# An encoder layer on one core: one x load on another queue, the squares of the next tile ahead of the scaling, and fillers re-dealt in the prelude

## The chip, the cores and the metric

The kernel runs on one core of a Trainium2 chip. A core has TensorE (matrix products and transposes, written into PSUM), VectorE and ScalarE (elementwise work and reductions), GpSimd (POOL in the profile) and SyncE (SP), which here only issues transfers. Transfers are issued on the queues of SP, ScalarE and GpSimd and are carried by 16 DMA engines. The metric is device time in microseconds for one launch, lower is better; for the kernel before it is the median of three runs.

## The reference

One layer over a sequence of 512 positions with 2048 features (`x`), conditioned on a vector `c`; all of it in float32:

```python
c_act = silu(c)
mod = c_act @ w_ada + b_ada                  # 2048 -> 3 x 2048
shift, scale, gate = split(mod, 3)
h = rms_norm(x, norm_gain) * (1 + scale) + shift
proj = h @ w_in                              # 2048 -> 7168: q, k, v, z of 8 attention and 4 retention heads
y = concat(attention(q, k, v) * silu(z), retention(q, k, v) * silu(z))
out = rms_norm(x + gate * (y @ w_out), final_gain)
```

`rms_norm` divides each position's 2048 features by the root of their mean square (plus 1e-6). The attention is a mixture of three dilated windows, the retention runs forward and backward.

## The kernel before

The 512 positions are four tiles of 128 (`t` = 0 to 3), the 2048 features 16 blocks of 128 (`k`). Products with weights run on TensorE at 32 bits in two parts: each operand is split into a rounded part and a rest, and three products (`mm3`, L89 and L91) stand for one.

The input projection needs h transposed, with features on the partitions. Features are taken in chunks of 1, 2, 2, 3, 4 and 4 blocks (`CHUNKS`); while TensorE multiplies one chunk with the weights, shift and scale of the next chunk are summed from w_ada on VectorE (`ada_pieces`, L204 and L208, loads at L197). For the first chunk, block 0 alone, there is nothing to hide this behind. That is the prelude, and the change lies in it.

The prelude does the following:

- Loads. The four x tiles (`xn`, 1 MB each; `xt` in the profile, L121) are issued on ScalarE's queue. `c`, `b_ada` and the gain go on GpSimd's. SP issues four pieces of w_ada for block 0 (`raw0`, L115, 0.5 MB each, in runs of 512 bytes), then the first weights of w_in (L510), then w_ada for the next chunk (L197).
- Fillers. `warm(n)` multiplies a square of ones with the identity n times (L353, two instructions each). The results are not used.
- Square sums. For tile t `squares_a(t)` squares the left 1024 features on ScalarE with a running sum (L300), `squares(t)` the right 1024 on VectorE (L305), adds the two sums (L308), and has GpSimd raise the mean to the power of -1/2 (L312).
- SiLU of c. `silu_c` (L271 to L275): a transpose on TensorE, the exponential on ScalarE, three operations on VectorE, the last of which writes `ct`.
- Scaling. `scaled(t, a, b)` multiplies features a to b of x tile t in place by that factor (L316, VectorE).
- Transposes. `k0_part(t)` transposes block 0 (L322, into `psk`), `turned(t, b)` four blocks (three where b = 0) into one PSUM bank (`psx`, L328), `evacuated(t, b, eng)` copies them out to `xT` (L336).
- Shift and scale of block 0. `sums0(b, i)` adds up eight products of a raw piece with `ct` (L286, 16 instructions with one column each, into `psa`); `turn_rows` transposes `b_ada` and the gain (L266) and copies them to `bg` (L267, L268); `shift_scale0` joins them (L293 to L295).
- h of block 0. `h0_sum` and `h0_low` (L345 to L349) write its two parts, and the first projection product can start (`pw`, L89).

The order on each engine is written out by hand: every instruction passed through `pin` keeps, on its engine, its place in program order. What isn't pinned is placed by a planner, which also orders the loads of the queues and shares the completion semaphores out among them. An engine's queue is in order: an instruction that waits, the issue of a load included, holds all that follow on that engine.

Of the kernel before, what the change touches and what calls it, by code (L numbers as in the profile page):

```python
# [17 lines left out]
P = 128  # L18
D = 2048
S = 512  # L20
NT = S // P
# [15 lines left out]
N_PERSIST = 2  # L37
ADA_SPAN = 0.65
TAB_SPAN = 16
WARM = 8, 6, 5, 6  # L40
LAG = 3
RAW, RAW1, WB, LOOK, LEAD, LEAD1, EB, YB = 3, 3, 3, 2, 4, 8, 1, 22
GR = 2
# [6 lines left out]
def trunk_kernel(ctx, tc, x, c, norm_gain, w_ada, b_ada, w_in, w_out, dec_f, dec_b, final_gain, out):  # L50
    nc = tc.nc
    x2, o2 = x[0], out[0]
# [9 lines left out]
    def bank(pool, nm):  # L62
        return pool.tile([P, 512], F32, tag="b", name=nm)
# [48 lines left out]
    xn = [xp.tile([P, D], F32, name=f"xt{t}") for t in range(NT)]  # L112
# [5 lines left out]
        )  # L118

    for t in range(NT):  # L120
        nc.scalar.dma_start(xn[t], x2[t * P : (t + 1) * P, :])  # L121
    nc.gpsimd.dma_start(c_row, c.rearrange("b (k p) -> (b k) p", p=P))
    for i in range(2):
        for b in range(2):
# [23 lines left out]
    pin = tc.keep_in_program_order  # L148
# [114 lines left out]
    bg = const.tile([P, 48], F32, name="bg")  # L263

    def turn_rows():
        pin(nc.tensor.transpose(ps0[:, 64:112], bg_row, ident[0:48, 0:48]))  # L266
        pin(nc.vector.tensor_copy(bg, ps0[:, 64:112]))  # L267
        pin(nc.vector.tensor_scalar_add(bg[:, 16:32], bg[:, 16:32], 1.0))  # L268

    def silu_c():  # L270
        pin(nc.tensor.transpose(ps0[:, 0:NK], c_row, ident[0:NK, 0:NK]))  # L271
        pin(nc.scalar.activation(ce, ps0[:, 0:NK], AF.Exp, scale=-1.0))
        pin(nc.vector.tensor_scalar_add(ce, ce, 1.0))
        pin(nc.vector.reciprocal(ce, ce))
        pin(nc.vector.tensor_tensor(ct, ps0[:, 0:NK], ce, op=ALU.mult))  # L275
# [3 lines left out]
    ps0 = bank(psA, "ps0")  # L279
# [3 lines left out]
    def sums0(b, i):  # L283
        for a in range(8 * i, 8 * i + 8):
            pin(
                nc.tensor.matmul(  # L286
                    psa[:, b : b + 1], raw0[b][:, a, :], ct[:, a : a + 1],
                    start=a + b == 0, stop=a == NK - 1, skip_group_check=True,
                )
            )  # L290

    def shift_scale0():
        pin(nc.vector.tensor_tensor(sv[:, 0:1], psa[:, 0:1], bg[:, 0:1], op=ALU.add))  # L293
        pin(nc.vector.tensor_tensor(av[:, 0:1], psa[:, 1:2], bg[:, NK : NK + 1], op=ALU.add))
        pin(nc.vector.tensor_tensor(av[:, 0:1], av[:, 0:1], bg[:, 32:33], op=ALU.mult))  # L295


    def squares_a(t):
        sa = aap.tile([P, 2048], F32, tag="araw", name="sqa", bufs=AR)
        marks["sq"] = pin(nc.scalar.activation(sa[:, 0:1024], xn[t][:, 0:1024], AF.Square, accum_out=ssx[:, t, 0:1]))  # L300

    def squares(t):
        sd = aap.tile([P, 1024], F32, tag="aacc", name="sqd")
        v = xn[t][:, 1024:2048]
        pin(nc.vector.tensor_tensor_reduce(sd, v, v, 1.0 / D, EPS, ALU.mult, ALU.add, ssx[:, t, 1:2]))  # L305
        ms = small.tile([P, 1], F32, tag="ms1", name="ms1", bufs=2)
        pin(
            nc.vector.scalar_tensor_tensor(  # L308
                ms, ssx[:, t, 0:1], 1.0 / D, ssx[:, t, 1:2], op0=ALU.mult, op1=ALU.add
            )  # L310
        )
        nc.gpsimd.tensor_tensor(rsx[:, t : t + 1], ms, mhalf[:, 0:1], op=ALU.pow)  # L312

    def scaled(t, a, b):
        v = xn[t][:, a:b]
        marks["sc"] = pin(nc.vector.tensor_scalar_mul(v, v, rsx[:, t : t + 1]))  # L316
# [3 lines left out]
    def k0_part(t):  # L320
        o = psk3[:, 0:P] if t == 3 else psk[:, t * P : (t + 1) * P]
        pin(nc.tensor.transpose(o, xn[t][:, 0:P], ident))  # L322

    def turned(t, b, pin=pin):
        ps = psx[t, b] = bank(psP, "psx")
        for j in range(b == 0, 4):
            k = 4 * b + j
            pin(nc.tensor.transpose(ps[:, j * P : (j + 1) * P], xn[t][:, k * P : (k + 1) * P], ident))  # L328

    def evacuated(t, b, eng):  # L330
        for i, g in enumerate(groups):
            lo, hi = max(g[0], 4 * b), min(g[-1] + 1, 4 * b + 4)
            if i and lo < hi:
                dst = xt_tiles[i][:, lo - g[0] : hi - g[0], t * P : (t + 1) * P]
                src = psx[t, b][:, (lo - 4 * b) * P : (hi - 4 * b) * P].rearrange("p (k f) -> p k f", k=hi - lo)
                marks[eng] = pin(eng(dst, src))  # L336

    act, dve = nc.scalar.copy, nc.vector.tensor_copy
# [12 lines left out]
    def warm(n):  # L351
        for _ in range(n):
            pin(nc.tensor.matmul(ps0[:, 128:256], ones, ident, start=True, stop=True))  # L353

    warm(WARM[0])
    squares_a(0)
    squares(0)
    silu_c()
    for t in range(NT):
        scaled(t, 0, P)  # L360
        k0_part(t)
        if t == 3:
            break
        scaled(t, P, 1024)
        turned(t, 0)
        turned(t, 1)
        squares_a(t + 1)
        squares(t + 1)
        if t < 2:
            warm(WARM[1 + t])  # L370
        if t == 0:
            turn_rows()
        else:
            sums0(t - 1, 0)
        evacuated(t, 0, act)
        evacuated(t, 1, act)
    for t in range(3):
        scaled(t, 1024, D)
        turned(t, 2)
        turned(t, 3)  # L380
        evacuated(t, 3, act)
        if t:
            evacuated(t - 1, 2, dve)
# [2 lines left out]
    evacuated(2, 2, dve)  # L386
    marks["conv1"] = [marks[act], marks[dve]]
    sums0(1, 1)
    warm(WARM[3])
    shift_scale0()  # L390
    A, B = slice(0, 3 * P), slice(3 * P, S)
    h0_sum(A, psk[:, A])
# [869 lines left out]
```

## Time and profile before

| | |
|---|---|
| median of three runs | 981.01 us (980.26 to 981.70) |
| the profiled execution | 980.83 us, of which the span of instructions is 979.1 us |
| TensorE busy (products / weight loads) | 949.8 / 828.9 us of the span |
| VectorE, ScalarE, GpSimd busy | 615.6, 374.5, 12.3 us |
| DMA | 141.49 MB, 145 GB/s over the span |
| mean granted TensorE clock | 0.985 |

The profile is that of one execution. Times in it count from the first instruction. A group's row has its line in the kernel, the engine, the operation, `output<-inputs` by the names of the program, the shapes and a count. In timelines the first two numbers are start and length, and brackets hold the idle time of the engine before the row and what ended it; `ACTq` or `SPq` is an engine's sequencer issuing a load. The chain of waits follows the work that ended last back in time, from each step to what released it. The granted clock is the share of TensorE's full clock that it was given. The page divides the span into 40 slices of 24.5 us; the prelude lies in the first two of them, so it is read in finer windows.

### The profile page before, as it was taken

To read this page: it belongs to the slowest core of one execution; us is meant where nothing else is said; L and a number is where in the kernel's file an instruction comes from. 1 tells how busy PE (TensorE), PEld (TensorE's weight loads), DVE (VectorE), ACT (ScalarE), POOL (GpSimd) and SP (SyncE) were. 2 spreads that over 40 slices of the span, in tenths; PEclk is the share of its full clock that TensorE was granted. 3 is DMA by queue.
4 is the path that set the end of the run, shared out by engine and by line. 5 is a ranking of instruction groups with operands and counts; after the bars stand their busy time and mean duration, and the time that the engine had idled before them with its cause. 6 is when DMAs were issued, how large, how long until landed. Compare 5 with 4: busy or idle time off the path is not lost.

```text
span 979.1 us, 14412 instructions
## 1 busy us (share of the span) xinstructions
PE 949.8 (97%) x5614; PEld 828.9 (85%) x5614; DVE 615.6 (63%) x1079; ACT 374.5 (38%) x738; POOL 12.3 (1%) x25
## 2 busy tenths in 40 slices
PE   3999899999999999999999999999999999999996
PEld 3978689787988888988998899998899988888896
DVE  1689998966968786565565556745534472535444
ACT  2374334325236554454343232422333372333321
POOL 1000000000000000000000000000000000000001
PEclk7799999999999999999999999999999999999998
DMA  9498879732562222212224625426322148234304
GB/s 332 137 298 276 291 236 327 255 105 92 170 200 80 65 66 86 65 44 86 66 76 140 210 70 173 150 66 214 109 65 89 64 162 290 86 116 142 108 1 172
DMA packets 108803, 141.49 MB, mean 145 GB/s; under 512 B 5640, under 2 KB 78008, under 8 KB 108224
## 3 DMA queue, kind: packets, MB, share of 16 engines
q1 hardware_dynamic: 106912, 134.26, 41.8%
q10 hardware_dynamic: 1728, 6.29, 1.7%
q8 instruction: 44, 0.72, 0.3%
q14 instruction: 23, 0.19, 0.1%
q0 software_dynamic: 96, 0.03, 0.0%
HBM read 136.36 MB, written 4.20 MB: 144 GB/s over the span
## 4 chain that ended last, share of the span: by engine, by line
PE 90%; DMA 4%; DVE 3%; issue 1%; ACT 1%; POOL 0%; SPq 0%; POOLq 0%; DVEq 0%; ACTq 0%
PE pp L91 24%; PE pw L91 15%; PE pp L89 12%; PE po L91 12%; PE pw L89 8%; PE po L89 6%; PE op L91 3%; PE sp L91 2%; DMA graw<-in_w_ada_dram 2%; PE op L89 2%; PE tp L721 1%; DMA raw<-in_w_ada_dram 1%; PE sp L89 1%; PE psx L328 1%; PE psa L286 1%
## 5 line engine op out<-in xcount | busy, mean ns | idle before, releaser
L489 ACT CAST whi<-raw 128x512 fp32r<-128x512 f32 (+1 forms) x289 | 175.0, 607 | 433.2 <-PE pp L91 197.8
L490 DVE TENSOR_TENSOR wlo<-raw,whi 128x512 fp32r<-128x512 f32 (+1 forms) x289 | 193.8, 671 | 212.4 <-ACT whi L489 207.8
L91 PE MATMUL pp<-wlo,hh 128*128 128x256 f32 x576 | 161.8, 281 | 0.6 <-DVE wlo L490 0.6
L89 PE MATMUL pp<-whi,hh 128*128 128x256 f32 x576 | 162.4, 282 | 0.0
L91 PE MATMUL pp<-whi,hl 128*128 128x256 f32 x576 | 161.4, 280 | 0.0
L89 PEld LDWEIGHTS pp<-whi,hh 128*128 128x128 f32 x576 | 108.4, 188 | 2.5 <-ACT sc L790 1.7
L91 PEld LDWEIGHTS pp<-wlo,hh 128*128 128x128 f32 x576 | 108.5, 188 | 1.6 <-DVE wlo L490 0.8
L91 PEld LDWEIGHTS pp<-whi,hl 128*128 128x128 f32 x576 | 108.4, 188 | 0.0
L89 PE MATMUL pw<-hh,whi 128*128 128x512 f32 x256 | 102.8, 402 | 2.4 <-DVE acc L893 1.3
L89 PE MATMUL pp<-hh,whi 128*128 128x512 f32 x256 | 101.6, 398 | 0.6 <-DVE kl L621 0.4
L91 PE MATMUL pw<-hh,wlo 128*128 128x512 f32 x256 | 101.6, 397 | 0.0
L91 PE MATMUL pp<-hh,wlo 128*128 128x512 f32 x256 | 101.5, 396 | 0.0
L91 PE MATMUL pp<-hl,whi 128*128 128x512 f32 x256 | 101.0, 394 | 0.0
L91 PE MATMUL pw<-hl,whi 128*128 128x512 f32 x256 | 100.7, 395 | 0.0
L91 PE MATMUL po<-wlo,yh 128*128 128x512 f32 (+1 forms) x252 | 92.6, 367 | 0.0
L89 PE MATMUL po<-whi,yh 128*128 128x512 f32 (+1 forms) x252 | 92.5, 367 | 0.0
L91 PE MATMUL po<-whi,yl 128*128 128x512 f32 (+1 forms) x252 | 92.5, 367 | 0.0
L208 DVE SCALAR_TENSOR_TENSOR aacc<-araw,ct,aacc 128x512 f32<-128x512 f32 (+2 forms) x75 | 75.9, 1012 | 3.5 <-DMA araw<-in_w_ada_dram 2.2
L893 DVE TENSOR_TENSOR acc<-acc,pw 128x512 f32<-128x512 f32 x100 | 66.8, 681 | 8.0 <-PE pw L91 7.6
L946 DVE SCALAR_TENSOR_TENSOR gacc<-graw,ct,gacc 128x512 f32<-128x512 f32 x60 | 44.9, 749 | 38.4 <-DMA graw<-in_w_ada_dram 37.8
L89 PEld LDWEIGHTS pw<-hh,whi 128*128 128x128 f32 x256 | 48.1, 188 | 17.8 <-DVE acc L893 4.5
L89 PEld LDWEIGHTS pp<-hh,whi 128*128 128x128 f32 x256 | 48.1, 188 | 14.1 <-ACT e L666 0.9
(227 smaller groups left out, 1573.1 us busy)
## 6 DMA issues: line engine op xcount, KB each, us to landing
raw<-in_w_in_dram SPq DMA_DIRECT2D x94, 512.0 KB, 3.7
araw<-in_w_ada_dram SPq DMA_DIRECT2D x48, 512.0 KB, 6.4
graw<-in_w_ada_dram SPq DMA_DIRECT2D x64, 256.0 KB, 2.9
raw<-in_w_out_dram SPq DMA_DIRECT2D x32, 512.0 KB, 3.5
raw<-in_w_in_dram SPq DMA_DIRECT2D x16, 384.0 KB, 3.6
araw<-in_w_ada_dram SPq DMA_DIRECT2D x16, 384.0 KB, 4.9
xt<-in_x_dram ACTq DMA_DIRECT2D x4, 1024.0 KB, 8.3
res<-in_x_dram SPq DMA_DIRECT2D x16, 256.0 KB, 6.0
```

The lines of the kernel that those rows point to most:

```text
L89: nc.tensor.matmul(o, lh, rh, start=start, stop=False, skip_group_check=True)
L91: nc.tensor.matmul(o, a, b, start=False, stop=stop and b is (rl if swap else rh), skip_group_check=True)
L208: ins = nc.vector.scalar_tensor_tensor(acc[:, :, :n], rv[:, a], ct[:, kr + a : kr + a + 1], acc[:, :, :n], op0=ALU.mult, op1=ALU.add,)
L286: nc.tensor.matmul(psa[:, b : b + 1], raw0[b][:, a, :], ct[:, a : a + 1], start=a + b == 0, stop=a == NK - 1, skip_group_check=True,)
L328: pin(nc.tensor.transpose(ps[:, j * P : (j + 1) * P], xn[t][:, k * P : (k + 1) * P], ident))
L489: c1 = nc.scalar.copy(dh, src)
L490: c2 = nc.vector.tensor_tensor(dl, src, f32(dh), op=ALU.subtract)
L721: nc.tensor.transpose(tp_[:, j * P : (j + 1) * P], pt[:, j * P : (j + 1) * P], ident)
L893: nc.vector.tensor_tensor(accs[u][i], accs[u][i], ps[i], op=ALU.add)
L946: nc.vector.scalar_tensor_tensor(st["acc"], raw, ct[:, kr : kr + 1], st["acc"], op0=ALU.mult, op1=ALU.add)
```

## The change

Four edits in the prelude, and nothing behind it:

- The second x tile is loaded on SP's queue, ahead of all that SP issued before, and no longer on ScalarE's.
- `squares` is cut in two: the squaring keeps the name, the joining of the sums and the power become `factor`. In the written order the squares of a tile now stand between `factor` and the scaling of the tile before it. The right half of tile 0 and the first block of tile 3 are scaled at the end of the third turn, before the last transposes, and the evacuations of a tile come right behind its transposes.
- The two VectorE instructions of `turn_rows` are no longer pinned.
- The fillers are five groups (9, 4, 8, 4, 4) in place of four (8, 6, 5, 6): the second now stands behind the SiLU, ahead of the first scaled tile; the third and fourth stand behind the transposes of tiles 0 and 1; the last again ahead of the shift and scale.

```diff
-WARM = 8, 6, 5, 6
+WARM = 9, 4, 8, 4, 4
...
     for t in range(NT):
-        nc.scalar.dma_start(xn[t], x2[t * P : (t + 1) * P, :])
+        (nc.sync if t == 1 else nc.scalar).dma_start(xn[t], x2[t * P : (t + 1) * P, :])
...
         pin(nc.tensor.transpose(ps0[:, 64:112], bg_row, ident[0:48, 0:48]))
-        pin(nc.vector.tensor_copy(bg, ps0[:, 64:112]))
-        pin(nc.vector.tensor_scalar_add(bg[:, 16:32], bg[:, 16:32], 1.0))
+        nc.vector.tensor_copy(bg, ps0[:, 64:112])
+        nc.vector.tensor_scalar_add(bg[:, 16:32], bg[:, 16:32], 1.0)
...
         pin(nc.vector.tensor_tensor_reduce(sd, v, v, 1.0 / D, EPS, ALU.mult, ALU.add, ssx[:, t, 1:2]))
+
+    def factor(t):
         ms = small.tile([P, 1], F32, tag="ms1", name="ms1", bufs=2)
...
     squares_a(0)
     squares(0)
     silu_c()
-    for t in range(NT):
+    warm(WARM[1])
+    squares_a(1)
+    factor(0)
+    squares(1)
+    for t in range(3):
         scaled(t, 0, P)
+        scaled(t, P, 1024)
+        factor(t + 1)
+        if t == 2:
+            scaled(0, 1024, D)
+            scaled(3, 0, P)
+        else:
+            squares_a(t + 2)
+            squares(t + 2)
         k0_part(t)
-        if t == 3:
-            break
-        scaled(t, P, 1024)
         turned(t, 0)
         turned(t, 1)
-        squares_a(t + 1)
-        squares(t + 1)
-        if t < 2:
-            warm(WARM[1 + t])
+        evacuated(t, 0, act)
+        evacuated(t, 1, act)
         if t == 0:
+            warm(WARM[2])
             turn_rows()
         else:
+            if t == 1:
+                warm(WARM[3])
             sums0(t - 1, 0)
-        evacuated(t, 0, act)
-        evacuated(t, 1, act)
+    k0_part(3)
     for t in range(3):
-        scaled(t, 1024, D)
+        if t:
+            scaled(t, 1024, D)
         turned(t, 2)
...
-    warm(WARM[3])
+    warm(WARM[4])
     shift_scale0()
```

## The prediction

> **What bounds the kernel now.** I read the page first (span 979.1 us, TensorE busy 97% of it), then the chain of waits of the stretch that the change touches, in order of time: start, length, what.
>
> ```profile
> 1.24 13.37 DMA raw<-in_w_ada_dram
> 14.61 0.02 issue
> 14.63 0.34 ACTq L121
> 14.97 0.03 issue
> 15.00 1.28 ACT L300
> ...
> 44.12 0.90 PE psx L328 x7
> ```
>
> The prelude ends where that last row ends and the first projection matmul follows, at 45.0 us. Behind it TensorE is nearly always busy, so the prelude's length is paid in full. Its first third is strange: the chain runs through a load of w_ada to an issue on ScalarE's queue, although ScalarE's first work is to square x. The timeline of that queue, in two pieces:
>
> ```profile
> 0.74 1.40 ACTq L121 DMA_DIRECT2D xt<-in_x_dram  x3
> 14.63 0.34 ACTq L121 DMA_DIRECT2D xt<-in_x_dram  x1
> ```
>
> And VectorE's, with what ended the idle time before each row:
>
> ```profile
> 6.00 1.23 DVE L305 CUSTOM_DVE_ANT_0 sqd<-xt 128x1024 f32<-128x1024 f32 x1 [5.12 <-DMA xt<-in_x_dram]
> ...
> 17.48 0.16 DVE L308 SCALAR_TENSOR_TENSOR ms<-ssx 128x1 f32<-128x1 f32 x1 [10.24 <-ACT sqa L300]
> ...
> 18.11 0.17 DVE L275 TENSOR_TENSOR ct<-ps,ce 128x16 f32<-128x16 f32 x1
> 18.39 0.88 DVE L316 TENSOR_SCALAR xt<-xt,rsx 128x128 f32<-128x128 f32 x2
> 19.18 1.22 DVE L305 CUSTOM_DVE_ANT_0 sqd<-xt 128x1024 f32<-128x1024 f32 x1
> 20.33 0.08 DVE L305 DVE_READ_ACCUMULATOR2_ANT ssx<- 128x1 f32 x1
> ...
> 23.95 0.21 DVE L267 COPY bg<-ps 128x48 f32<-128x48 f32 x1 [3.28 <-PE ps L266]
> ...
> 27.22 0.88 DVE L316 TENSOR_SCALAR xt<-xt,rsx 128x128 f32<-128x128 f32 x2 [0.66 <-POOL rsx L312]
> ```
>
> Three x tiles are issued by 2.14. The fourth is held until 14.63, when the second raw load has landed, and everything on ScalarE is queued behind that issue. VectorE has its half of tile 0 at 6.00 and then waits 10.24 us for ScalarE's half. Why a load of x waits for one of w_ada: in the trace's issue records the loads of the two queues take eight completion semaphores in turn, and the fourth x load is the first there to reuse one still in flight.
>
> From 19.3 us TensorE, in the order written, carries the prelude. Its timeline:
>
> ```profile
> 19.32 1.76 PE L328 MATMUL psx<-ident,xt 128*128 128x128 f32 x7
> 20.87 2.77 PE L353 MATMUL ps<-ident,ones 128*128 128x128 f32 x12
> 23.57 0.34 PE L266 MATMUL ps<-ident,bg_row 48*128 48x48 f32 x1
> 24.61 0.33 PE L322 MATMUL psk<-ident,xt 128*128 128x128 f32 x1 [0.70 <-DVE xt L316]
> 25.21 0.99 PE L328 MATMUL psx<-ident,xt 128*128 128x128 f32 x7 [0.26 <-DVE xt L316]
> 26.03 1.28 PE L353 MATMUL ps<-ident,ones 128*128 128x128 f32 x10
> 27.15 1.84 PE L286 MATMUL psa<-ct,raw 128*128 128x1 f32 x16
> ...
> 29.76 2.63 PE L286 MATMUL psa<-ct,raw 128*128 128x1 f32 x16
> 32.26 0.45 PE L322 MATMUL psk<-ident,xt 128*128 128x128 f32 x1
> ...
> 37.54 3.81 PE L286 MATMUL psa<-ct,raw 128*128 128x1 f32 x32
> ```
>
> The same time by stretches (length, PE busy, granted clock, DMA share, GB/s):
>
> ```profile
> 24.60:30.70 6.10, 5.83 (x51) 0.99 1.09 348
> 30.70:37.40 6.70, 6.70 (x33) 0.50 0.43 135
> 37.40:40.90 3.50, 3.50 (x34) 0.99 0.00 0
> ```
>
> Prices from start to start: a filler product 0.225 us at clock 0.5 (2.70 for 12), 0.11 at 1.0 (1.12 for 10); a transpose 0.21 at 0.5 (5.28 for the 25 from 32.26), 0.117 at 1.0. The clock changes in steps of some 3.4 us (30.7, 37.4, 40.9): down after a step rich in `psa` products, which have one column each, up after one full of transposes.
>
> **The x tile on SP's queue.** ScalarE's queue now issues three loads. In the issue records two raw loads (1 MB) stand between x loads 1 and 2, two between 2 and 3, three w_in loads (1 MB) between 3 and 4: the planner orders the two queues by bytes. By that rule the last x load now comes sixth or seventh, among the first eight, and waits for nothing. ScalarE is free at 2.14, and its 1.28 us table load fits before x arrives (if it too waits for x: +1.28, in the range).
>
> The price is that x tiles 0 and 1 travel together. GB/s is the last column:
>
> ```profile
> 10.00:11.00 1.00, 0.00 (x0) 0.00 (x0) 0.00 (x0) 0.00 (x0) 0.00 (x0) 0.57 1.00 402
> 11.00:12.00 1.00, 0.00 (x0) 0.00 (x0) 0.00 (x0) 0.00 (x0) 0.00 (x0) 0.50 1.04 299
> ```
>
> A tile of 1.05 MB takes 2.6 us at 402 GB/s. Tile 0 had landed at 6.0, so tiles 1 and 2 at about 8.6 and 11.2, just where the rate falls to 299 and w_ada alone is left. Now tile 0 lands between 6.0 (served in order of issue) and 8.6 (shared evenly with tile 1). I take 8.6, since two queues have equal claims; tile 2 then lands at 11.2, tile 3 at 13.8. Behind tile 1 SP has four raw, six w_in and six araw loads, all 2.6 us later at first: the second raw at 17.2 instead of 14.6, the fourth, two times 1.8 us on (0.52 MB at 299), at 20.8. Their users, the `psa` products, come to them at 20 us and later: hidden. The bytes are the same, so DMA still ends near 33.3 (135 GB/s over 6.7 us is 2.6 us at 348), before the loop starts.
>
> The Trainium skill (DMA: Bandwidth & Descriptors, Issuing engines are not separate DMA queues) holds that loads of all issuing engines share 16 DMA engines, so that spreading them saves only issue time. For the bytes I count the same; the 12.5 us ahead of the fourth issue are not issue time. What the rule alone would give is rival (b).
>
> **Reordered squares.** From 8.6: ScalarE's half takes 1.2 (15.00 and 1.28 to 17.48), to 9.8; silu's chain to `ct` 0.8 more; `factor(0)` 0.16, 10.8; `squares(1)`, 1.30 with its read, now ahead of the scaling: 12.1, where it was 18.39. That 1.30 hides POOL's power and is repaid, since the 0.66 wait per tile goes: 0.88 + 0.16 + 1.30 + 0.1 = 2.4 us from one scaling to the next. So 12.1, 14.5, 16.9, and tile 3's first columns, behind tile 0's right half, before 19. `squares_a` ahead of the evacuations costs ScalarE 1.2 a tile, under TensorE's fillers.
>
> **bg out of the written order.** Its copy made VectorE wait 3.28. Wherever the planner puts it, it costs VectorE 0.4 to 3.7; TensorE comes to tile 1 at 18.5, 3 us after VectorE is ready, so nothing. Without that cover, up to 3.
>
> **Fillers.** 9, 4, 8, 4, 4 for 8, 6, 5, 6, two products each. The first two groups run before x is there; then 16 products for 12 and 8 for 10.
>
> **The sum on TensorE**, at the clock that each row had: first `psx` 0.93 after the scaling, 13.05; 7 transposes 1.55, 16 fillers 3.6, bg 0.25: 18.45. Tile 1: 8 transposes 0.94, 8 fillers 0.9; sums and tile 2's transposes 2.61 (27.15 to 29.76): 22.9. Sums 2.50, 25 transposes 5.28, 32 products 3.81: 34.5, against 41.35. That takes over the 6.7 us at half clock. If the steps keep their places (17.0, 20.4, 23.8, 27.2, 30.6), the dense fillers raise the clock at 17.0, the sums lower it at 23.8, the transposes fill one step and raise it at 27.2, and only the last sums, from 30.6, are slowed again: 33.0. With full clock from 17 on it is 28. I take 33.0, 8.35 earlier. From there to the loop it takes the same 3.7 us, but 8 fillers cover less of it than 12, and the loop may begin with a microsecond at half clock: minus 0.45. Gain 7.9. The profiled run took 980.83 (1.73 around its span), the median of the runs is 981.01: 972.9 and 973.1, I say 973.0.
>
> The Trainium skill (TensorE: Matmul & The Clock Gate, Part 4) says that transposes don't bring the full clock. Here the 25 transposes are followed by 0.99; what the page would make of it is rival (e).
>
> **Rivals.**
> (a) ScalarE stays held: the last x load still stands behind the second raw load, which now lands at 17.2. Table load to 18.9, ScalarE's half 20.1, scaling 0 after silu and `squares(1)` at 22.3, and 0.9 + 21.45 (13.05 to 34.5) later the last sum, 44.7: 3.3 slower, 984.3. It decides as soon as that load is ninth or later in the shared turn. For it: it was so before. Against: the order by bytes.
> (b) Only one issue's time, 0.45, is saved: scaling 0 at 19.3, last sum 41.7: 981.3, no change. Against: the wait's length.
> (c) The loop meets its loads late and gives half back: 977. For: DMA runs without pause to 33. Against: SP then waited for VectorE to free buffers, up to 13.5 us at once, so the loop's loads follow the loop:
>
> ```profile
> SPq L510 <- DVE wlo L490: 16.6, 4, 13.5
> ```
>
> (d) Half clock throughout: 48 transposes and 64 products at 0.21, 24 fillers at 0.225, bg: 29.2, last sum 42.3: 981.9. Against: 12 fillers at 20.87 were followed by 0.99.
> (e) The clock lowered at 23.8 stays low, transposes or not: 25 and 32 times 0.21 from 23.9, last sum 35.9: 976. Against: the rows of 30.70 and 37.40.
>
> **Numbers.** Forecast 0.78, (a) 0.06, (b) 0.03, (c) 0.06, (d) 0.04, (e) 0.03. The forecast's own spread runs from 967.5 (full clock from 17 us on) to 976.5 (table load behind x, one more step at half clock); with (c) and (e) the range is 967.5 to 977.5. 0.2%, 2 us, is about what a measurement of this kernel tells from no change: faster 0.87 (forecast, c, e), same 0.07 (b, d), slower 0.06 (a).
>
> **What would show it.** Right: table load near 2.2 us, ScalarE's squares at 8 to 9, no w_ada load in the chain before 15 us, scalings 2.4 us apart without a wait for POOL, last `psa` near 33, first projection near 36.5. Wrong: an x issue on ScalarE's queue after 10 us (a, b); TensorE waiting for loads between 36 and 60 us (c); clock 0.5 for most of 13 to 33 us (d) or from 24 us to the last sum (e).

## The result, and the profile after

The kernel after takes 973.07 us (median; its runs took 971.82 to 973.56), against 981.25 us (980.26 to 981.70) for the kernel before, measured beside it: a ratio of 0.9916, with a 95% interval of 0.9899 to 0.9933. The profiled execution took 973.0 us with a span of 971.2 us, 7.9 us shorter than before. That is the predicted time; the steps to it hold less well.

Where the 7.9 us come from is seen first in the chain of waits of the kernel after (start, length, what):

```profile
0.74 8.18 DMA xt<-in_x_dram
...
11.17 1.41 POOL rsx L314
...
13.55 1.76 PE psx L330 x7
...
18.46 0.22 DVE bg L267
...
29.10 4.58 PE psa L286 x32
...
37.08 0.43 PE pw L89
```

No load of w_ada is left in it. The first `psx` transposes start at 13.55 us instead of 19.32, the last `psa` product ends at 33.67 instead of 41.35, and the loop is reached at 37.08 by this chain, 7.9 us earlier. ScalarE's timeline shows what let go:

```profile
2.29 1.28 ACT L300 ACT_TABLE_LOAD   x1 [2.29 <-issue]
8.95 1.06 ACT L300 ACTIVATE sqa<-xt 128x1024 f32<-128x1024 f32 x1 [5.38 <-DMA xt<-in_x_dram]
```

The table load at 2.29, behind three issues (15.00 before), and then a wait for the data alone. VectorE and GpSimd in the same stretch:

```profile
10.93 1.22 DVE L305 CUSTOM_DVE_ANT_0 sqd<-xt 128x1024 f32<-128x1024 f32 x1
12.07 0.08 DVE L305 DVE_READ_ACCUMULATOR2_ANT ssx<- 128x1 f32 x1
12.61 0.88 DVE L318 TENSOR_SCALAR xt<-xt,rsx 128x128 f32<-128x128 f32 x2 [0.45 <-POOL rsx L314]
...
18.46 0.21 DVE L267 COPY bg<-ps 128x48 f32<-128x48 f32 x1 [3.76 <-PE ps L266]
18.70 0.17 DVE L268 TENSOR_SCALAR bg<-bg 128x16 f32<-128x16 f32 x1
18.79 0.87 DVE L318 TENSOR_SCALAR xt<-xt,rsx 128x128 f32<-128x128 f32 x2
```

```profile
11.17 1.40 POOL L314 TENSOR_TENSOR rsx<-ms,mhalf 128x1 f32<-128x1 f32 x1 [7.47 <-DVE ms L310]
...
22.33 0.99 POOL L314 TENSOR_TENSOR rsx<-ms,mhalf 128x1 f32<-128x1 f32 x1 [1.06 <-DVE ms L310]
```

Two things came otherwise than forecast. The power, now beside VectorE's squares, takes 1.40 us, and VectorE still waits 0.45 us for it. And the copy to `bg`, no longer pinned, was placed ahead of the scaling of tile 1, so that VectorE waits 3.76 us for the transpose behind 16 fillers. TensorE pays for that, as its timeline shows:

```profile
15.10 3.13 PE L355 MATMUL ps<-ident,ones 128*128 128x128 f32 x16
18.16 0.26 PE L266 MATMUL ps<-ident,bg_row 48*128 48x48 f32 x1
19.12 0.33 PE L324 MATMUL psk<-ident,xt 128*128 128x128 f32 x1 [0.70 <-DVE xt L318]
19.72 0.99 PE L330 MATMUL psx<-ident,xt 128*128 128x128 f32 x7 [0.27 <-DVE xt L318]
...
21.43 1.84 PE L286 MATMUL psa<-ct,raw 128*128 128x1 f32 x16
...
25.90 1.91 PE L330 MATMUL psx<-ident,xt 128*128 128x128 f32 x16
```

It idles 0.70 and 0.27 us ahead of tile 1, as long as in the kernel before (0.70 and 0.26), where the copy stood at the same place. From there to 31.2 us it runs at the full clock, the sums of 21.43 and the transposes of 25.90 alike (length, PE busy, granted clock, DMA share, GB/s):

```profile
14.00:18.00 4.00, 4.00 (x23) 0.55 1.21 291
...
22.00:26.00 4.00, 4.00 (x38) 1.00 1.06 370
26.00:30.00 4.00, 3.77 (x36) 1.00 1.09 348
30.00:34.00 4.00, 4.00 (x25) 0.65 0.91 290
34.00:38.00 4.00, 4.00 (x18) 0.50 0.22 70
```

The clock rises at about 17.6 us (the first row has 3.6 us at 0.50 and 0.4 at 1.00), falls at about 31.2 within the last `psa` products, and is back to full at 38. Behind the prelude the program is the same, so the sums of the next chunk are a fixed mark, first in the kernel before, then after:

```profile
L222 PE MATMUL psm<-ones,aacc x8: 250/250/271, 61.9 to 62.8; 128*128 128x1 f32 x8
```

```profile
L222 PE MATMUL psm<-ones,aacc x8: 250/250/271, 54.5 to 55.3; 128*128 128x1 f32 x8
```

From the first of them to the end it is 917.2 us before and 916.7 after, and 916.1 to 918.5 in every profile below. So 7.4 of the 7.9 us lie ahead of this mark, and the 0.5 us behind it is less than the 2.4 us by which the profiles differ there.

### The profile page after: what moved, and what is told of

It reads as the page before. It is cut to its first block, busy times and chain, and to the rows that moved or that the text cites. A ratio compares the mean times of both kernels' runs of the same rounds, so it can differ in the third digit from the quotient of the medians.

```text
span 971.2 us, 14425 instructions
## 1 busy us (share of the span) xinstructions
PE 950.2 (98%) x5622; PEld 829.0 (85%) x5622; DVE 615.2 (63%) x1079; ACT 374.8 (39%) x738; POOL 15.4 (2%) x25
## 4 chain that ended last, share of the span: by engine, by line
PE 84%; DVE 6%; DMA 6%; issue 2%; ACT 1%; POOL 0%; SPq 0%; POOLq 0%; DVEq 0%; ACTq 0%
PE pp L91 24%; PE pw L91 12%; PE po L91 12%; PE pp L89 12%; PE pw L89 6%; PE po L89 6%; PE op L91 3%; DMA araw<-in_w_ada_dram 2%; PE sp L91 2%; DMA graw<-in_w_ada_dram 2%; DVE aacc L208 2%; PE op L89 2%; PE tp L733 1%; PE sp L89 1%; DVE wlo L502 1%
```

## The experiments

Ratios are to the kernel before, on the same chip in the same session, with 95% intervals.

**The x tile alone.** In the kernel before:

```diff
-        nc.scalar.dma_start(xn[t], x2[t * P : (t + 1) * P, :])
+        (nc.sync if t == 1 else nc.scalar).dma_start(xn[t], x2[t * P : (t + 1) * P, :])
```

> The kernel before with one edit: x tile 1 on SP's queue. The order of squares and scalings, the pinned bg copy and the fillers are as before. My theory (ScalarE was held by its fourth x issue) expects the table load near 2.3 us, ScalarE's squares at 8.9, the first scaling near 11.0 instead of 18.4, the last psa product at 33.5 to 34.5 instead of 41.35, and about 974 us (972 to 977), so nearly the whole gain. The rival that the reordered squares and the new fillers are needed for the gain expects more than 978. The rival that only issue time is saved expects 981.

973.41 us (971.51 to 976.30) against 983.23: 0.9903 [0.9876, 0.9930]. This one line gives the whole gain. The table load waits for nothing:

```profile
2.28 1.28 ACT L300 ACT_TABLE_LOAD   x1 [2.28 <-issue]
```

The first scaling starts at 11.32 us, 1.3 us earlier than in the kernel after, since `squares(1)` does not stand ahead of it, and the power takes 0.56 us, beside SiLU's three short operations.

**The rest alone.** In the kernel after, all four x loads back on ScalarE's queue, so that the new order and the new fillers remain.

> The kernel after with the x tile put back: all four x loads on ScalarE's queue, squares ahead of the scaling, bg not pinned, fillers 9, 4, 8, 4, 4. My theory expects the fourth x issue held until 14.6 us as in the kernel before, the first scaling 1.6 us later than in the kernel before (near 20.0, since silu and the squares of tile 1 now stand ahead of it), then the 20.1 us from the first psx to the last psa product that the kernel after takes: last product near 41, time 980.5 (979 to 982.5), no change. The rival that the order and the fillers carry the gain expects less than 977.

978.29 us (977.51 to 978.54) against 983.23: 0.9949 [0.9934, 0.9964]. ScalarE is held as before:

```profile
0.74 14.60 ACTq L121 DMA_DIRECT2D xt<-in_x_dram  x4
15.37 1.28 ACT L300 ACT_TABLE_LOAD   x1 [15.37 <-DMA raw<-in_w_ada_dram]
```

The first transposes start 1.9 us later than before, at 21.26, as was to be expected with more work ahead of them. They run at half speed (1.76 us for seven, as at 19.32 in the kernel before), but from 23.5 us to 40.6 everything runs at the full clock, the second sums and the transposes behind them too:

```profile
30.92 1.84 PE L286 MATMUL psa<-ct,raw 128*128 128x1 f32 x16
...
32.77 1.91 PE L330 MATMUL psx<-ident,xt 128*128 128x128 f32 x16
```

So the kernel is faster than the kernel before, where no change was expected: from the first `psx` to the last `psa` it takes 18.2 us, not the 20.1 of the kernel after. Together the two halves should then have given 9.8 + 4.9 us; they gave 8.2, and 9.3 when the kernel after was measured again.

**Why ScalarE was held: the load, not the queue.** In the kernel before, all x loads stay on ScalarE's queue, and the four pieces of w_ada for block 0 become two of 1 MB:

```diff
-    for i in range(2):
-        for b in range(2):
-            load0(nc.sync, b, i)
+    for b in range(2):
+        load0(nc.sync, b, 0)
```

(`load0` now fetches all of `raw0[b]`.)

> The kernel before, all four x loads on ScalarE's queue and the old order, but the raw pieces of w_ada in two loads of 1 MB instead of four of 0.5 MB, so that the last x load is the ninth in the shared turn and reuses the semaphore of x tile 0. My theory (the hold is the semaphore shared with a raw load) expects the fourth x issue at about 6.2 us, when tile 0 has landed, instead of 14.6, the table load right behind it, the first scaling near 10, the last psa product near 32.5 to 34, and about 973 us (971 to 976). The rival that a load must leave ScalarE's queue, or that SP's queue brings the gain, expects 981, with the fourth issue still after 14 us.

973.11 us (971.77 to 974.49) against 983.23: 0.9898 [0.9880, 0.9916]. The chain of waits:

```profile
0.74 6.52 DMA xt<-in_x_dram
7.28 0.33 ACTq L121
```

The fourth x load is now the ninth of the shared turn and waits for the first x tile instead of a raw load: it is issued at 7.28 us instead of 14.63. The whole gain comes without any load on another queue. So it was the shared completion semaphore that held ScalarE, as the first step of the prediction said.

**The copy to bg.** In the kernel after, the copy and its addition are pinned behind `factor(3)`, as `copy_rows`:

```diff
         if t == 2:
+            copy_rows()
             scaled(0, 1024, D)
```

> The kernel after with the two bg instructions written out behind factor(3), ahead of the scaling of tile 0's right half, so that VectorE no longer waits 3.8 us for the bg transpose ahead of scaling tile 1. If that wait costs TensorE its 0.97 us of idle time before tile 1's transposes, scaling 1 comes near 15.2 instead of 18.8, the last psa product near 32.7 instead of 33.7, and the time is 972.0. If the steps of TensorE's clock take it back, or VectorE's wait is hidden as I forecast, it stays at 973.0.

973.29 us (970.09 to 974.27) against 983.23: 0.9903 [0.9885, 0.9921]. In the profile tile 1 is scaled at 15.00 us instead of 18.79, TensorE does not idle ahead of it, and the last `psa` ends at 31.10. Not all of these 2.6 us are the copy's: the clock rose at 14.5 us in this execution, 3 us earlier than in the first profile of the kernel after. The times don't tell the two kernels apart. Its GpSimd shows the power in both settings:

```profile
16.03 1.46 POOL L316 TENSOR_TENSOR rsx<-ms,mhalf 128x1 f32<-128x1 f32 x1 [1.06 <-DVE ms L312]
18.55 0.55 POOL L316 TENSOR_TENSOR rsx<-ms,mhalf 128x1 f32<-128x1 f32 x1 [1.06 <-DVE ms L312]
```

1.46 us beside the squares, 0.55 us with VectorE idle, then at the short copy to `bg`.

**The kernel after once more, and the x tile alone once more**, both unchanged, side by side.

> The kernel after, unchanged, as the measure beside the next three. 0.9916 of the kernel before was measured; a ratio of 0.990 to 0.993 is expected. If its times spread by the step of TensorE's clock that the prelude meets, runs with a lower mean clock are the longer ones.

> Again the kernel before with x tile 1 on SP's queue and nothing else, now beside the kernel after. If the reordered squares and the re-dealt fillers add nothing once x is moved, its ratio to the kernel before lies within 0.002 of that of the kernel after. If they add what they brought alone (0.5%), it lies 0.004 or more above.

973.49 us (970.64 to 975.24), 0.9913 [0.9893, 0.9933], for the kernel after; 973.49 us (970.01 to 977.09), 0.9909 [0.9885, 0.9934], for the x tile alone. Once the tile is moved, the new order and fillers add nothing that these runs could show. The profile of the kernel after differs from its first one in a single thing, the clock (two rows of TensorE's timeline, then two windows):

```profile
13.57 1.76 PE L330 MATMUL psx<-ident,xt 128*128 128x128 f32 x7
15.12 2.22 PE L355 MATMUL ps<-ident,ones 128*128 128x128 f32 x16
```

```profile
10.00:14.00 4.00, 2.85 (x11) 1.00 1.02 384
...
30.00:34.00 4.00, 4.00 (x31) 0.84 0.94 295
```

The 1.00 of the first window is no reading. The trace's record of the clock begins at 15.7 us here, and the view shows what lies ahead of it as full. The seven transposes of 13.57 took the 1.76 us that they took in the first profile at 0.50, so they ran at half speed. The 16 fillers behind them took 2.22 us instead of 3.13: the clock rose at 15.7 us instead of 17.6. It fell at 32.8 instead of 31.2, the last `psa` ended at 31.67 instead of 33.67, and the run took 970.64 us. The six runs order themselves nearly by their mean granted clock (970.64 at 0.996 to 975.24 at 0.988). Those of the tile alone do not (970.01 at 0.992, 973.12 at 0.995), and what lies ahead of a record counts as full in these means.

**Without the fillers behind the transposes.** In the kernel after:

```diff
-WARM = 9, 4, 8, 4, 4
+WARM = 9, 4, 0, 0, 4
```

> The kernel after without the two groups of fillers behind the transposes of tiles 0 and 1 (9, 4, 0, 0, 4). If the fillers bring TensorE's clock up at 17 us and earn their 4 us by it, the transposes and psa products up to about 27 us run at half clock (spacing 0.21 instead of 0.11), the last psa product comes at 34 to 35 instead of 33.7, time 973.5 to 975. If they only cost their own time, the last product comes near 31 and the time is 970.5.

976.49 us (973.30 to 977.95) against 982.83: 0.9936 [0.9916, 0.9956], 3.0 us more than the kernel after beside it; the intervals overlap, but five of the six runs are longer than every run of the kernel after. Tile 1 is reached 2.8 us earlier, at 16.35, and the loop 2.2 us later, because nearly everything up to 31 us runs at half clock (a row of TensorE's timeline, then two windows):

```profile
27.03 4.74 PE L330 MATMUL psx<-ident,xt 128*128 128x128 f32 x24
```

```profile
26.00:30.00 4.00, 4.00 (x20) 0.50 1.09 348
30.00:34.00 4.00, 4.00 (x35) 0.87 0.92 290
```

So in this profile the fillers pay through the clock. Without them it is only the 24 transposes that bring it up, at about 31 us.

**The new order with the old fillers**, all x loads on ScalarE's queue:

```diff
-WARM = 9, 4, 8, 4, 4
+WARM = 8, 0, 6, 5, 6
```

> The kernel after with all x loads on ScalarE's queue and the fillers as near as can be to those of the kernel before (8, none, 6, 5, 6): the new order alone. If the 0.5% of the order with its fillers came from the fillers, which filled a whole step of the clock, the ratio to the kernel before is 0.998 to 1.003. If the order itself brings it, the ratio stays at 0.995.

983.09 us (981.65 to 986.44) against 980.96: 1.0026 [1.0006, 1.0045]. What the rest alone had gained was the fillers' doing; the order by itself, with ScalarE held, brings nothing and may cost a little. One window over the last sums and what follows, of this kernel and then of the one with the new fillers:

```profile
38.00:42.00 4.00, 4.00 (x21) 0.51 0.00 0
```

```profile
38.00:42.00 4.00, 4.00 (x30) 0.82 0.08 11
```

**Other ways to the same end.** Three more variants of the kernel after: the first group of fillers longer; the x tiles 0, 1 and 2 on ScalarE's queue and tile 3 on SP's behind the first two raw loads, with `copy_rows`; and the latter with 14 fillers at first.

```diff
-WARM = 9, 4, 8, 4, 4
+WARM = 20, 4, 8, 4, 4
```

> The kernel after with 20 fillers instead of 9 in the first group, so that TensorE stays busy until about 9.5 us, while x is still on its way, and meets tile 0 at 13.5 us with the clock still up. If the step at which the clock comes up (15.5 or 17.3 us in the two profiles of the kernel after) makes the spread of its runs, the first seven transposes come every 0.11 us instead of 0.22, the last psa product comes at 31 to 32 in every run, the median is 971 and the runs lie closer together. If the clock falls in the gap of 9.5 to 13 us all the same, the time is that of the kernel after, 973.5.

```diff
-    for t in range(NT):
-        (nc.sync if t == 1 else nc.scalar).dma_start(xn[t], x2[t * P : (t + 1) * P, :])
+    for t in range(3):
+        nc.scalar.dma_start(xn[t], x2[t * P : (t + 1) * P, :])
...
             load0(nc.sync, b, i)
+        if i == 0:
+            nc.sync.dma_start(xn[3], x2[3 * P : 4 * P, :])
```

> The kernel with the late bg copy, but x tiles 0, 1 and 2 on ScalarE's queue and tile 3 on SP's, behind the first two raw loads. Tile 0 has ScalarE's queue for itself beside small packets and should land at 6.0 as in the kernel before instead of 8.8, all eight loads still have a semaphore of their own, and tile 3 comes near 17, before its squares are due. If the arrival of tile 0 sets the prelude, the first scaling comes at 9.8 instead of 12.5, the loop starts 2.7 us earlier, and the time is 970.5, the best of all. If TensorE's clock or tile 3 takes it back, it stays at 973.

> The kernel with x tile 3 behind the first raw loads and the late bg copy, with 14 fillers instead of 9 in the first group, up to about 8.2 us. Its tile 0 is transposed from 12.1 us on. With the clock held up its last psa product comes near 30.5 instead of 32.2 and the time is 969.5; if the clock falls near 10 us all the same it stays at 971.2.

971.20 us (969.67 to 973.98), 0.9896 [0.9869, 0.9923]; 971.22 us (970.83 to 972.51), 0.9889 [0.9870, 0.9908]; 971.47 us (969.92 to 973.33), 0.9895 [0.9870, 0.9921]. All three ratios lie about 0.2% under the kernel after, and all three intervals overlap its own, so none is shown to be better. With 20 fillers the first transposes start 1.1 us later, at 14.66 (the fillers hold up SiLU's transpose), and the loop still starts at 33.71, since the clock is full from 8.9 to 32.8 us. The runs lie no closer together for it, 4.3 us against 4.6. With tile 1 off SP's queue, tile 0 lands at 7.1 us instead of 8.9, not at the 6.0 of the kernel before; why not is open. The rest alone, which issues its x loads as the kernel before does, also had it at 7.1, so it need not be tile 3. The first scaling then waits for the squares of tile 1, which lands at 10.0. Fourteen fillers on top gave nothing, though they held the clock up to 20.7 us.

**The last sums taken apart.** By then the profiles seemed to agree in one thing: where the granted clock fell, `psa` products had filled a large part of the 3.4 us ahead (2.5 us in the kernel before, at 30.6). The bound of 1.9 us that the expectation below states does not hold. With steps of 3.4 us laid from where the record shows a change, and products counted from start to start, the steps after 15 us in which the clock stayed up held up to 2.06 us of them (kernel after, up to 24.4) and those followed by a fall 2.05 us (bg late, up to 28.2) or more. One step ahead of a fall held only 1.8 us (14 fillers, up to 20.7), with TensorE idle for 0.4 us of it. In the kernel after:

```diff
         if t:
             evacuated(t - 1, 2, dve)
-    sums0(0, 1)
+        if t == 1:
+            sums0(0, 1)
+    warm(4)
     scaled(3, P, 1024)
```

> The kernel after with the last two groups of sums taken apart: sums0(0, 1), 16 psa products, stands behind the transposes of tile 1 instead of tile 2, and four more fillers (8 products) stand behind the transposes of tile 2, ahead of sums0(1, 1). Theory: the clock is changed in steps of some 3.4 us, and a step in which psa products fill about 1.9 us or more is followed by half clock, one with 1.7 us or less is not. In the two profiles of the kernel after, the one step that had more (1.9 and 2.5 us, within the last 32 products) was followed by half clock, and the steps with 1.7 us were not. Here the last three groups of 16 products (1.68 us each) have 1.8 us or more between them, so no step there can hold more than 1.7 (the first two groups are 0.93 us apart as before, and a step that took in parts of both could still lower it): the clock stays at full from 26 us until the first projection product; last psa 0.9 us (the new fillers) behind the 31.7 that a profile with a full clock gave, so near 32.5, first projection product 2 us later, near 34.5; median 1 to 2 us below the 973.3 of the kernel after, ratio near 0.990. Rival: the clock falls by its own count, whatever the share of psa products in a step (or at any such product): half clock again somewhere from 26 to 34 us, last psa at 33.5 or later, first projection product at 36.5 or later, and a time equal to the kernel after or up to 1 us above it.

The last sums are now two rows in TensorE's timeline, and the clock no longer falls:

```profile
26.19 1.84 PE L286 MATMUL psa<-ct,raw 128*128 128x1 f32 x16
...
29.69 1.84 PE L286 MATMUL psa<-ct,raw 128*128 128x1 f32 x16
```

```profile
30.00:34.00 4.00, 3.73 (x31) 1.00 0.98 306
34.00:38.00 4.00, 3.28 (x19) 1.00 0.16 54
```

The step with the most `psa` products, up to 24.9 us, held 1.9 us of them. The first projection product starts at 33.57 us, in spite of eight more filler products. Six of the seven runs took 969.65 to 971.90 us, at clocks of 0.994 to 0.998 (0.988 to 0.996 in the kernel after); the seventh took 980.67 at 0.984, which leaves the ratio at 0.9906 [0.9872, 0.9941] against a kernel before of 980.38. The profile came out as the theory said and not as its rival did. But the edit takes the sums apart and adds fillers in one, so it doesn't tell whether the one-column products lower the clock or only leave too little other work in a step. The steps lie at another place in each execution, so one profile is one draw. That the edit makes the kernel faster is not shown.

## Why the prediction was right, and where its steps failed

The time from the first transposes to the first projection product says it best. All are starts in the profiled executions, in us, from TensorE's timelines:

| kernel | first `psx` | first `pw` | between |
|---|---|---|---|
| before | 19.32 | 44.77 | 25.5 |
| after, first and second profile | 13.55, 13.57 | 36.74, 33.62 | 23.2, 20.1 |
| x tile alone, first and second | 12.26, 11.96 | 39.98, 37.40 | 27.7, 25.4 |
| raw loads in two | 11.96 | 37.27 | 25.3 |
| rest alone | 21.26 | 41.32 | 20.1 |
| new order, old fillers | 21.01 | 44.62 | 23.6 |
| without fillers behind transposes | 13.62 | 38.91 | 25.3 |
| bg late | 13.40 | 34.16 | 20.8 |
| last sums apart | 13.45 | 33.57 | 20.1 |

The first column is set by ScalarE and the order: moving the tile brings it 7.1 to 7.7 us forward in either order, and the new order takes 1.3 to 1.9 us of that back. The third goes with the clock, and so in part with the fillers: from 28 us, mostly at half clock, to 20. The parts don't add because the order that starts later is also the one with the denser TensorE. In the medians the two effects cancel. The profiles have the kernel after 3 to 4 us ahead of the tile alone, but each is one execution: the slowest of four for the tile alone, the fastest of six for the kernel after measured again. Runs of the tile alone spread by 7 us, so whether the order and the new fillers earn a microsecond or two once the tile is moved stays open.

Step by step:

- **The x tile on SP's queue**: right, in cause and size. Raw loads in two shows the cause, the shared semaphore, apart from the queue. Rivals (a) and (b) are out by the table load at 2.29.
- **Tile 0 at 8.6**, shared evenly with tile 1: it landed at 8.9. The later raw loads cost nothing, as said.
- **Reordered squares**: the step "that 1.30 hides POOL's power and is repaid, since the 0.66 wait per tile goes" failed. The power takes 1.40 to 1.47 us beside the squares and ends 0.42 us after them (12.57 against 12.15), so a wait of 0.43 to 0.45 remains. The first scaling came at 12.61 instead of 12.1. The Trainium skill has a reason that the prediction missed (SBUF — State Buffer, Who interferes with whom): a VectorE instruction with two inputs in SBUF contends with a GpSimd instruction that reads SBUF. The squares read `v` twice, and the rows of 1.46 and 0.55 agree with it. The 0.99 us beside a scaling, which reads one tile, is not covered by that sentence, and no run here takes the two inputs apart.
- **bg out of the written order**: the step "TensorE comes to tile 1 at 18.5, 3 us after VectorE is ready, so nothing" failed. The planner put the copy ahead of the scaling of tile 1, and the transpose that it waits for stands behind the same 16 fillers that were to hide its wait. It cost 0.97 us of idle TensorE in the profile, as much as in the kernel before, where the pin held it at that place.
- **The clock**: "the dense fillers raise the clock at 17.0" was right (17.6, and 15.7 in the second profile). "The sums lower it at 23.8" was wrong: it stayed up until 31.2. The prediction took any step rich in `psa` products to lower it. In the kernel before, most of two groups of 16 products fell into the step of 27.2 to 30.6, 2.5 us of it; after, one group and the start of the next, 2.06 us, fell into the step of 21.0 to 24.4. So the second sums took 1.70 us instead of 2.50 and the 25 transposes 3.2 instead of 5.28, and rival (e), which lived on that fall, is out too, like (d).
- **The sum**: sums began at 21.43 instead of 20.3 (0.5 late at the first transposes, the rest ahead of tile 1, where TensorE idled 0.97). From there to the last products it took 7.5 us, where the items, at a clock that falls, add to 10.4, and the last products took 4.7 instead of 3.81: 33.7 against 33.0. To the loop it then took 3.4 us, where 3.7 was taken, and the loop began with 1.3 us at half clock, where one was taken. So the forecast time rests on one right large term and on errors of a microsecond or more that cancelled. The second profile, 2 us shorter at the end of the sums, shows how far luck went.
- **The lower end of the range**: "with full clock from 17 on it is 28" is a slip in the sum. By the prediction's own prices (0.11 a filler, 0.117 a transpose, 1.7 us for 16 `psa` products) it is about 30.3, and the time 970 instead of 967.5. The second profile, at full clock from 15.7 to 32.8 us, had 31.67 and 970.64.
- **Rival (c)**, the loop meeting its loads late: out: TensorE waits for no load between 36 and 62 us, and from the fixed mark on it is 916.7 us.

## What to carry to other kernels

An issue that waits holds its whole engine, so when an engine's first work starts late, look at what ends the wait of the issue ahead of it: here a completion semaphore shared with a load on another queue, which could be freed by moving one load or by issuing one load fewer, for 1% of the kernel. Fillers are to be judged by the clock they leave behind, not by the time they take or cover. A pin that is taken off is only free if the work that is to cover the wait is not itself queued behind what is waited for.

## What was not expected of the hardware

- GpSimd's power of 128x1 elements took 0.55 us alone, 0.99 us beside a scaling and 1.40 to 1.47 us beside VectorE's squares, and in the kernel after it ended 0.40 to 0.42 us after VectorE's instruction each time.
- The same kernel met its clock steps at different places: full from 15.7 us in one execution, from 17.6 us in another, with 2 us between their last `psa` products. A granted clock of 1.00 ahead of the first entry in the record is not to be trusted: products there came at half speed.
- Steps of 3.4 us filled with products of one column were followed by half clock, although TensorE never idled in most of them: 2.05 us or more of such products went ahead of a fall, 2.06 us or less did not, but for one step with 1.8 us and a pause. Taking the last groups apart, with fillers between them, kept the clock at full. The bound itself was not tried.
- 24 transposes at half clock were followed by the full clock (no fillers, 27.03 us). The Trainium skill (TensorE: Matmul & The Clock Gate, Part 4) says that the full clock does not engage for transposes; the measurement differs.
